# A decoder trunk with three attention groups on one core: a new order of mixing's steps, and joint slots for values and MLA results

## The chip, the core and the metric

The kernel runs as one program on one core of one Trainium2 chip. The metric is the device time of that program in microseconds (us), weights and input in device memory at its start, the result there at its end. Times of several runs are given as a median with the least and the greatest.

## What is computed

The input is 512 tokens of 1024 features in float32, and there are two layers. Each layer normalises its input, projects it once, and hands the columns to three groups of heads. The three outputs (512 + 256 + 256 features) go into one output projection, which is added to the input; an MLP of width 4096 with a squared ReLU follows, and after the last layer a final norm.

```python
for l in range(DEPTH):                                   # 2
    h = rmsnorm(x, g_mix[l])
    (cq, ckv, kr, aq, ak, av, qi, ki, wi, rq, rk, rv, rg) = jnp.split(h @ w_in[l], split_at, axis=-1)
    # MLA, 8 heads: low-rank queries (768) and keys/values (256), a shared rotary key, causal softmax
    q  = rmsnorm(cq, g_q[l]) @ w_uq[l]                   # 8 x (64 + 32 rotary)
    kv = rmsnorm(ckv, g_kv[l]) @ w_ukv[l]                # 8 x (64 key + 64 value)
    o_a = mla_attention(q_nope, q_rope, k_nope, k_rope, v_mla)
    # DSA, 4 heads, one key/value head: an indexer's score picks 128 causal keys per query
    score = einsum('bqh,bqhk->bqk', wi * idx_scale, relu(q_i . k_i))
    o_b = softmax over the keys of top_k(score, 128)
    # retention, 4 heads: decayed scores, group norm, swish gate
    o_c = silu(rg) * head_groupnorm(retention(q_c, k_c, rv), g_ret[l])
    x = x + concatenate([o_a, o_b, o_c]) @ w_out[l]
    x = x + square(relu(rmsnorm(x, g_mlp[l]) @ w_ff1[l])) @ w_ff2[l]
return rmsnorm(x, g_final)
```

## The kernel before

**Tiles.** Activations lie transposed, features on the 128 partitions and the 512 tokens along the free dimension, so a tile is 128x512 float32. Where the precision of float32 is wanted, a value is kept as a pair (high part and rest, both fp32r), and a product is three matmuls (`mm3`, the matmul itself at L146): high by high, rest by high and high by rest. Weights come from memory by DMA (tag "wr"), and `wsplit` makes the pair: ACT or POOL copies the high part (L192, L194), DVE or POOL subtracts (L215, L217). `gemm` is such a product over a list of contraction tiles, with the sum in one PSUM bank of tag "mm" (three of them); scores have three banks ("sc"), the products with values two ("o"). SBUF slots are shared by tag: 13 "g", 8 "qk", 8 pairs "u", 6 "p", 2 "v", one "sm". A tile of a tag waits until the slot's earlier tile has its last reader behind it.

**Who sets the order.** The kernel's Python emits instructions in program order, and a scheduler of the tile framework puts each on its engine's list by priority and by the readiness that it computes; `hp(k)` lowers or raises that priority for a kind of work by the table `PRI` (top-k rounds -225, results of the MLA -70, retention -44, `dm` +8, and so on). Program order in the mixing half of a layer is the string `ORDER`, whose words one loop hands to functions. The words are:

- `qi`, `tk`, `ix`: indexer queries, token tiles, index scores; they end in `accs`, three tables of 256, 384 and 512 keys. `t n` takes the next n jobs of the top-k queue: 48 rounds (`top_round`, L760 takes eight maxima, L761 replaces them; three tables, 16 rounds each), then three masks (L765).
- `rq`, `rk`, `rg`, `r n`: retention's queries, keys and gate, and the next n of its 16 scores.
- `aq`: DSA's queries. `dm` (`dsa_max`, scores L146, maxima L1110): the greatest score of each query and head over the masked keys; a transpose (L1114) and two small DMAs put it into a row of the queries, from which the exponentials are later taken. `d0` to `d3` (`dsa_block`, exponential L1159, results from L1133): the DSA blocks of 128 queries. They write `mix[4]` and `mix[5]`; retention writes `mix[6]` and `mix[7]`.
- `kv`, `kvf`, `kvc`: low-rank keys and values, their norm factor (L914) and the conversion. `cq`, `cqf`: low-rank queries and their factor. `mk`: slots of the keys, with the rotary key.
- `v0`, `v1` (`round_v`, copies out of PSUM L972): values of four heads each, from slots of tag "v". `rr0`, `rr1` (`round_rope`): the rotary part of a round's queries: a gemm, L978, a swap by DMA (L308), products (L143), a sum, a split.
- `k`, `q` (`pair_k`, `pair_q`): keys and queries of a pair of heads. The queries leave PSUM at L998, and four small DMAs (L1004) bring the rotary part of each head out of what `rr` left.
- `m` (`pair_max`, maxima L1025 and L1032): the greatest score of each query, as in `dm`.
- `a0` to `a7` (`pair_attn`, exponential L1093): one head each, four blocks of keys. The product with the values of a block is held back (`push`, four may be pending) so that scores go ahead of it; `F` flushes what is pending. When a pair's second head is done, `pair_done` copies the sums and products out of PSUM (L1050, L1052), takes the reciprocal by logarithm and exponential (L356, L357), corrects it, and writes the pair of `mix[gp]` (L1068) into a slot of tag "qk".

After the string comes OUT, the output projection: eight tiles of eight contraction tiles each, 192 matmuls, in the order 6, 7, 4, 5, 0, 1, 2, 3 of `mix`. The packing of the weight on the host (`mo`) has the same order. Then the MLP starts, for which the slots of "sm" and "v" are used too.

## Time and profile before

| | before |
|---|---|
| three runs, us | 1372.92, 1377.91, 1378.54 |
| median, us | 1377.91 |
| the profiled execution's own time, us | 1373.71 |
| its span, us | 1371.9 |
| mean granted clock of TensorE, of full | 0.979 |
| PE busy, us (7276 matmuls) | 1324.2 (97%) |
| weight loads (PEld) busy, us | 1100.4 (80%) |
| DVE busy, us (1744) | 1023.3 (75%) |
| ACT busy, us (1151) | 658.3 (48%) |
| POOL busy, us (263) | 268.9 (20%) |

The profile is of one execution; its starts and lengths are in us from the span's start. Its own time lies 1.8 us above its span. PE is TensorE's matmuls, DVE is VectorE, ACT is ScalarE, POOL is GpSimd, SP is the queue from which most DMAs are issued (SPq). Busy time of PE counts a matmul from its start to its modelled end, so two that follow each other overlap a little; the step from one start to the next is what it costs. [...]

### The profile page before, as it was taken

To read this page: it belongs to the slowest core of one execution; us is meant where nothing else is said; L and a number is where in the kernel's file an instruction comes from. 1 tells how busy PE (TensorE), PEld (TensorE's weight loads), DVE (VectorE), ACT (ScalarE), POOL (GpSimd) and SP (SyncE) were. 2 spreads that over 40 slices of the span, in tenths; PEclk is the share of its full clock that TensorE was granted. 3 is DMA by queue.
4 is the path that set the end of the run, shared out by engine and by line. 5 is a ranking of instruction groups with operands and counts; after the bars stand their busy time and mean duration, and the time that the engine had idled before them with its cause. 6 is when DMAs were issued, how large, how long until landed. Compare 5 with 4: busy or idle time off the path is not lost. (4 is left out here: it accounts for less than half of the span.)

```text
span 1371.9 us, 19881 instructions
## 1 busy us (share of the span) xinstructions
PE 1324.2 (97%) x7276; PEld 1100.4 (80%) x7276; DVE 1023.3 (75%) x1744; ACT 658.3 (48%) x1151; POOL 268.9 (20%) x263
## 2 busy tenths in 40 slices
PE   9999989999999999999998989899999999999997
PEld 7877765668888888899987767656778888889997
DVE  5799995555777776797759999756457776777875
ACT  4534433783444443465636345438644444445652
POOL 3456741004000000000033656311130000000000
PEclk9999997999999999999999998989999999999998
DMA  6668232203554555476555651221035555554652
GB/s 216 170 179 216 68 89 59 89 18 110 163 180 159 183 186 169 138 223 208 173 167 164 180 158 54 85 73 66 32 108 169 186 183 169 164 188 153 201 183 80
DMA packets 75777, 197.53 MB, mean 144 GB/s; under 512 B 8960, under 2 KB 13792, under 8 KB 75680
## 3 DMA queue, kind: packets, MB, share of 16 engines
q1 hardware_dynamic: 74528, 195.22, 46.1%
q8 instruction: 57, 0.93, 0.3%
q10 hardware_dynamic: 1152, 1.05, 0.2%
q14 instruction: 40, 0.33, 0.1%
HBM read 155.68 MB, written 20.97 MB: 129 GB/s over the span
## 5 line engine op out<-in xcount | busy, mean ns | idle before, releaser
L146 PE MATMUL mm<-u,wh 128*128 128x512 f32 (+1 forms) x1776 | 551.6, 390 | 0.0
L146 PEld LDWEIGHTS mm<-u,wh 128*128 128x128 f32 x1776 | 330.7, 189 | 64.6 <-issue 0.5
L146 PE MATMUL mm<-u,wl 128*128 128x512 f32 (+1 forms) x888 | 344.9, 388 | 0.1
L192 ACT ACTIVATE wh<-wr 128x512 fp32r<-128x512 f32 (+2 forms) x247 | 150.0, 610 | 296.9 <-PE mm L146 172.5
L215 DVE TENSOR_TENSOR wl<-wr,wh 128x512 fp32r<-128x512 f32 (+2 forms) x208 | 148.3, 714 | 84.1 <-ACT wh L192 83.1
L217 POOL TENSOR_TENSOR wl<-wr,wh 128x512 fp32r<-128x512 f32 (+2 forms) x80 | 102.9, 1287 | 489.5 <-ACT wh L192 405.5
L146 PEld LDWEIGHTS mm<-u,wl 128*128 128x128 f32 x888 | 167.8, 189 | 35.0 <-issue 0.7
L503 DVE TENSOR_TENSOR u<-wr,u 128x1024 fp32r<-128x1024 f32 x54 | 65.8, 1222 | 26.0 <-ACT u L502 25.8
L502 ACT ACTIVATE u<-wr 128x1024 fp32r<-128x1024 f32 x54 | 57.2, 1059 | 54.8 <-PE o L516 14.3
L445 DVE TENSOR_TENSOR sm<-wr 128x512 f32<-128x512 f32 x64 | 44.1, 690 | 47.5 <-DMA wr<-in_wff 47.5
L516 PEld LDWEIGHTS sc<-g,v 128*128 128x128 f32 x576 | 72.2, 189 | 2.3
L516 PE MATMUL sc<-g,v 128*128 128x256 f32 x576 | 73.1, 281 | 0.0
L146 PE MATMUL sc<-u,qk 97*128 97x512 f32 (+5 forms) x192 | 53.1, 393 | 3.6 <-ACT p L1093 3.6
L433 DVE SCALAR_TENSOR_TENSOR g<-mm,g 128x512 f32<-128x512 f32 x64 | 43.9, 686 | 14.7 <-PE mm L146 14.6
L194 POOL TENSOR_SCALAR wh<-wr 128x512 fp32r<-128x512 f32 (+3 forms) x41 | 28.9, 706 | 124.0 <-PE mm L146 60.5
L761 DVE MATCH_REPLACE8 g<-m,g 128x384 f32<-128x384 f32 (+2 forms) x96 | 51.3, 539 | 0.1
L342 PE MATMUL o<-p,v 128*128 128x256 f32 (+2 forms) x128 | 50.6, 499 | 0.0
L516 PE MATMUL o<-g,v 128*128 128x256 f32 x384 | 50.5, 281 | 0.0
L449 ACT ACTIVATE v<-wr 128x1024 fp32r<-128x1024 f32 x32 | 34.0, 1062 | 33.3 <-DVE wr L447 33.1
L760 DVE MAX8 m<-g 128x8 f32<-128x256 f32 (+2 forms) x96 | 49.9, 545 | 0.1
L516 PEld LDWEIGHTS o<-g,v 128*128 128x128 f32 x384 | 47.5, 189 | 0.0
L516 PE MATMUL sc<-wh,u 128*128 128x256 f32 x224 | 46.1, 285 | 0.8 <-DVE x L533 0.4
(299 smaller groups left out, 2631.8 us busy)
## 6 DMA issues: line engine op xcount, KB each, us to landing
wr<-in_wff SPq DMA_DIRECT2D x160, 512.0 KB
wr<-in_win SPq DMA_DIRECT2D x37, 512.0 KB
ws<-sm SPq DMA_DIRECT2D x32, 512.0 KB
wr<-ws SPq DMA_DIRECT2D x32, 512.0 KB
tab<-in_tabs SPq DMA_DIRECT2D x20, 512.0 KB
wr<-in_wout SPq DMA_DIRECT2D x16, 512.0 KB
p<-p SPq DMA_DIRECT2D x40, 128.0 KB
wr<-in_wuq SPq DMA_DIRECT2D x12, 384.0 KB
```

Source lines behind the costliest of these rows:

```text
L146: return nc.tensor.matmul(out, lhsT, rhs, start=start, stop=stop)
L192: return nc.scalar.activation(out, src, AF.Copy)
L215: order["wl"] = nc.vector.tensor_sub(lo, rc, R(hi))
L217: nc.gpsimd.tensor_sub(lo, rc, R(hi))
L342: nc.tensor.matmul(o[:, q0:], *terms[0], start=i == 0, stop=i == NB - 1, skip_group_check=True)
L433: nc.vector.scalar_tensor_tensor(r, ps, 0.0, rb, op0=ALU.max, op1=ALU.mult)
L445: nc.vector.tensor_add(sm[:, h], w[0], w[1])
L502: nc.scalar.activation(wh, t, AF.Copy)
L503: nc.vector.tensor_sub(wl, t, R(wh))
L516: nc.tensor.matmul(outs[m][0], a[:, m * P : m * P + P], b, start=i == 0 and outs[m][1] and n == 0, stop=i == KP - 1 and n == 2, skip_group ...
L760: nc.vector.max(m8, accs[j])
L761: nc.vector.match_replace(out=accs[j], in_to_replace=m8, in_values=accs[j], imm_value=GONE)
```

## The change

Three things change, and both layers have them. First, the string `ORDER`: the top-k jobs are handed out one or two at a time between the gemms, with what is left in one step behind `m2`; retention's scores come early; `aq1` and `aq0` stand behind `cq2`; `rr1`, `q2`, the heads `a2` and `a3` and `m2` stand ahead of `dm`; `dm` stands behind `k3` and directly ahead of `q3`; the DSA blocks come as `d3`, `d2`, `d1`, `d0` with the heads `a4`, `a5`, `a6` between them, and `a7` is last. Second, the slots: both rounds' values share one slot of tag "v"; the results of the first three MLA pairs share the other (`oss["mix"]`), and the fourth pair's goes to "sm". Third, OUT takes its contraction tiles in the order 6, 7, 0, 1, 2, 3, 4, 5, and the packed weight follows.

```diff
--- before.py
+++ after.py
@@ -51,7 +51,7 @@
 OPT_R = 0
 MHI = 'aaap'
 MLO = 'vp'
-ORDER = 'qi0 rg0 qi1 tk ix1 ix2 F rq0 ix3 rk0 rq1 r1 t2 r1 r1 t3 rk1 t4 rg1 aq1 r1 r1 aq0 F t2 t2 F F F F F t2 F F kv0 kv1 F F t1 F F r2 cq0 t2 t2 r1 r1 cq1 r4 kvf kvc t2 cq2 cq3 t5 r7 cq4 t1 t4 r16 t4 t2 cq5 r12 F F r6 r12 t1 F r2 v0 r16 r14 F r14 r9 cqf r2 t4 mk F t2 r1 r2 cqc r2 r2 r3 F t1 r11 rr0 t1 t4 t4 q0 r4 k1 t5 F k0 t2 r4 F t2 r2 q1 t4 r6 t4 r2 F t10 t10 t3 t4 m0 r2 r6 t2 r5 m1 r3 r2 r1 t3 t2 t5 a0 a1 t2 k2 t4 t4 dm t7 t4 r10 r1 t9 rr1 r1 t7 t3 r2 t4 a2 q2 a3 q3 t3 r3 m2 r7 t6 r10 r2 d2 t5 d3 d0 t15 d1 k3 t4 t2 r2 t2 t1 t3 m3 v1 a4 t8 t1 a6 F t3 r2 t4 t59 t2 r1 t6 r2 a7 r2 t3 t1 t3 a5 t2 t3 F r1 F r3 r2 r10 F r2 F'
+ORDER = 'qi0 rg0 qi1 tk ix1 ix2 F rq0 ix3 rk0 rq1 r1 r1 r1 rk1 rg1 t1 r1 r1 F kv0 kv1 t1 r2 cq0 t1 r1 r1 cq1 t1 r4 kvf kvc t1 cq2 t1 aq1 aq0 cq3 t1 r7 cq4 t1 cq5 t1 F cqf mk t1 v0 t2 rr0 t1 k0 t1 q0 t1 k1 t1 q1 t1 m0 t2 m1 t2 a0 t3 a1 t2 k2 t2 rr1 t2 q2 t3 a2 t3 a3 t3 m2 t59 k3 dm q3 d3 v1 m3 d2 a4 d1 a5 d0 a6 a7 F'
 PRI = {'fin': 0, 'w': 99, 'e': 59, 't': -225, 'rope': 0, 'split': 133, 'q': -16, 'qm': 0, 'rr': 0, 'v': 5, 'k': 0, 'att': 0, 'pv': 0, 'done': -70, 'ret': -44, 'st': 65, 'x': 0, 'tab': -20, 'cq': 0, 'tok': 15, 'idx': 0, 'dm': 8, 'rg': 0, 'km': 0, 'qi': 0, 'aq': 0}
 TOPK = 128
 NEG = -1e30
@@ -956,7 +956,10 @@
 
         def round_v(rd):
             with hp("v"):
-                v = v_([P, NB, 2, 192], F32)
+                if not vv:
+                    t = v_([P, 2, NB, 2, 192], F32)
+                    vv.update({"all": t})
+                v = vv["all"][:, rd]
                 for pr in range(2):
                     nc.gpsimd.memset(v[:, :, pr, 64:128], 1.0)
                 vv[rd] = v
@@ -1063,7 +1066,9 @@
                         rows = slice(64 * e, 64 * e + 64)
                         nc.vector.tensor_mul(y[rows], oss[gp, e][rows], y[rows])
                 nc.vector.scalar_tensor_tensor(s, s, 2.0, y, op0=ALU.subtract, op1=ALU.mult)
-                mt_ = qk_()
+                if gp == 0:
+                    oss["mix"] = v_([P, 3, 2, T])
+                mt_ = oss["mix"][:, gp] if gp < 3 else S("sm", 1, [P, 2, T], FR)
                 mh, ml = mt_[:, 0], mt_[:, 1]
                 nc.scalar.activation(mh, s, AF.Copy, scale=-1.0)
                 nc.vector.scalar_tensor_tensor(ml, s, -1.0, R(mh), op0=ALU.mult, op1=ALU.subtract)
@@ -1229,7 +1234,7 @@
             with after("aug") if OPT_X else nullcontext():
                 nc.sync.dma_start(x[n], xsrc[n])
         for n in range(KD):
-            ps = gemm(wout[l, n], (6, 7, 4, 5, 0, 1, 2, 3), mix)
+            ps = gemm(wout[l, n], (6, 7, 0, 1, 2, 3, 4, 5), mix)
             nc.vector.tensor_add(x[n], x[n], ps)
             sumsq_add(ss, x[n], n == 0, n == KD - 1)
         mode.update(hi="a", lo="v")
@@ -1334,7 +1339,7 @@
     wv = np.stack([f["w_ukv"][l][:, vcols].reshape(2, P, 2, 256).transpose(2, 1, 0, 3).reshape(2, P, 512)
                    for l in L])
     d["wukv"] = np.concatenate([wk, wv], 3)
-    mo = np.concatenate([np.arange(t * P, (t + 1) * P) for t in (6, 7, 4, 5, 0, 1, 2, 3)])
+    mo = np.concatenate([np.arange(t * P, (t + 1) * P) for t in (6, 7, 0, 1, 2, 3, 4, 5)])
     d["wout"] = np.stack([_pack(f["w_out"][l][mo]) for l in L])
     d["wff1"] = np.stack([_pack(f["w_ff1"][l]) for l in L])
     rows = np.concatenate([np.arange(t * P, (t + 1) * P) for t in (0, 1, 4, 5, 2, 3, 6, 7)])
```

The number of instructions on each engine is the same. A line of the kernel before at or behind L962 is 3 further on in the changed kernel, from L1069 on 5 (L998 is L1001 there). Where the new order moves them, three places show. Names are those of the program's tiles, with a running number that differs between the two; a row is line, operation, written tile <- read tiles, and shape of the moving or written data.

The first is PE in layer 0 inside `dm`. `sc` <- `km` is a DSA score, the matmul with `ma` and `cbt` behind it adds the mask; `mm` <- `x` or `u` is a product of queries. Before:

```order
L146 MATMUL sc_2252<-km_293,qk_1125 128x512
L146 LDWEIGHTS cbt
L146 MATMUL sc_2252<-ma_450_1941,cbt 128x512
L146 MATMUL sc_2256<-km_293,qk_1125 128x512
L146 LDWEIGHTS cbt
L146 MATMUL sc_2256<-ma_450_1941,cbt 128x512
L342 MATMUL o_2323<-p_2180,v_1785 128x256
L146 MATMUL sc_2260<-km_293,qk_1055 128x512
L146 LDWEIGHTS cbt
L146 MATMUL sc_2260<-ma_450_1941,cbt 128x512
L342 MATMUL o_2323<-p_2180,v_1785 128x256
```
And the change, at the fifth and sixth score since `dm`'s start and what follows; `mm_2498` is the sum of `q3`:

```order
L146 MATMUL sc_2438<-km_293,qk_1449 128x256
L146 LDWEIGHTS cbt
L146 MATMUL sc_2438<-ma_557_2402,cbt 128x256
L146 MATMUL sc_2438<-km_293,qk_1449 128x256
L146 LDWEIGHTS cbt
L146 MATMUL sc_2438<-ma_557_2402,cbt 128x256
L146 MATMUL mm_2498<-x_1191,wh_2490 128x512 x2
L146 MATMUL mm_2498<-x_1191,wl_2491 128x512
L146 MATMUL sc_2444<-km_293,qk_1395 128x256
L146 LDWEIGHTS cbt
L146 MATMUL sc_2444<-ma_557_2402,cbt 128x256
```
Before, scores and masks alternate, with a product of `p` and `v` (the first MLA heads) between; products of queries come at its end. Now six scores with their masks stand first, and from there three matmuls of `q3` come between scores.

The second is DVE in layer 0, at the end of the top-k rounds. `MAX` and `MATCH_REPLACE` are a round's two halves, the `tiny` rows are `pair_max`. Before, behind the first two evictions of queries (L998); the one instruction of these rounds that stands further ahead, between the evictions and this piece, is the `MAX` of `m_446`:

```order
L1025 TENSOR_REDUCE tiny_2098<-sc_2113 128x2
L1032 TENSOR_REDUCE tiny_2098<-sc_2119 128x1
L1032 TENSOR_REDUCE tiny_2098<-sc_2123 128x1
L215 TENSOR_TENSOR wl_2439<-wr_2436,wh_2438 128x384
L760 MAX m_447_1934<-g_761 128x8
L761 MATCH_REPLACE g_666<-m_446_1931,g_666 128x384
L761 MATCH_REPLACE g_761<-m_447_1934,g_761 128x512
L765 TENSOR_SCALAR ma_449_1939<-g_666 128x384
L765 TENSOR_SCALAR ma_450_1941<-g_761 128x512
```
And the change, where L1001 is that eviction:

```order
L143 TENSOR_TENSOR p_1787<-p_1787 128x512
L765 TENSOR_SCALAR ma_557_2402<-g_624 128x256
L761 MATCH_REPLACE g_666<-m_555_2396,g_666 128x384
L761 MATCH_REPLACE g_761<-m_556_2399,g_761 128x512
L238 TENSOR_TENSOR g_1826<-p_1787,g_1825 128x512
L1001 TENSOR_TENSOR g_1881<-mm_1862,g_1714 128x512
L1001 TENSOR_TENSOR g_1947<-mm_1928,g_1714 128x512
L765 TENSOR_SCALAR ma_558_2404<-g_666 128x384
```
All rounds and one of the masks now stand ahead of the first two evictions; before, four halves of rounds and two masks stood behind them.

The third is PE in layer 0 where the output projection first stands. Before, `mm_2979` is its first sum:

```order
L146 MATMUL sc_2844<-u_2467,qk_1864 128x256 x2
L146 LDWEIGHTS cbt
L146 MATMUL sc_2844<-cbt 128x128
L146 MATMUL sc_2844<-u_2467,qk_1865 128x256
L342 MATMUL o_2835<-p_2798,v_2698 128x256 x2
L146 MATMUL mm_2979<-u_1456,wh_2971 128x512
L146 MATMUL sc_2852<-u_2467,qk_1864 128x256 x2
L146 LDWEIGHTS cbt
L146 MATMUL sc_2852<-cbt 128x256
L146 MATMUL sc_2852<-u_2467,qk_1865 128x256
L342 MATMUL o_2863<-p_2833,v_2698 128x512
```
And the change, where `mm_2616` is a sum of `v1`, and `mm_2976` and `mm_3013` are the first two sums of OUT, ahead of a score of the block d3 (`sc_2535`):

```order
L146 MATMUL mm_2616<-wl_2589,g_1344 128x256
L146 MATMUL mm_2616<-wh_2588,g_1345 128x256
L146 MATMUL mm_2976<-u_1300,wh_2968 128x512 x2
L146 MATMUL mm_2976<-u_1300,wl_2969 128x512
L146 MATMUL mm_2976<-u_1692,wh_2968 128x512 x2
L146 MATMUL mm_2976<-u_1692,wl_2969 128x512
L146 MATMUL mm_2976<-v_2284,wh_2968 128x512 x2
L146 MATMUL mm_2976<-v_2284,wl_2969 128x512
L146 MATMUL mm_3013<-u_1300,wh_3005 128x512
L146 MATMUL sc_2535<-qk_1450,km_293 128x256
L146 MATMUL sc_2535<-qk_1395,km_295 128x256
```
Before, one matmul of OUT stands among the scores of the fourth pair's first head (row `mm_2979`), and the rest behind the last head. Now 10 stand directly behind `v1` and 7 more among the scores of d3, ahead of the DSA blocks d2 to d0 and the fifth to eighth head.

## Rows read from the trace of the kernel before

**Rows 1.** The page: busy time by engine; granted clock in 40 slices, in tenths.
```profile
PE 1324.2 (97%) x7276; PEld 1100.4 (80%) x7276; DVE 1023.3 (75%) x1744; ACT 658.3 (48%) x1151; POOL 268.9 (20%) x263
...
PEclk9999997999999999999999998989999999999998
```

**Rows 2.** Stretches of mixing: us, busy time by engine, granted clock, DMA share, GB/s.
```profile
60.00:193.90 133.90, 121.67 (x534) 94.45 (x532) 132.08 (x268) 61.30 (x121) 84.85 (x81) 0.99 0.54 150
207.40:214.90 7.50, 7.50 (x43) 5.21 (x41) 3.84 (x10) 4.53 (x10) 0.00 (x0) 1.00 0.61 176
214.90:237.50 22.60, 22.60 (x57) 10.88 (x56) 11.58 (x18) 5.81 (x11) 4.16 (x5) 0.62 0.04 13
217.80:234.90 17.10, 17.10 (x33) 7.29 (x33) 7.58 (x12) 2.84 (x5) 0.00 (x0) 0.50 0.05 16
237.50:250.90 13.40, 13.40 (x76) 9.48 (x75) 7.14 (x12) 6.70 (x16) 0.98 (x2) 1.00 0.52 167
250.90:305.00 54.10, 50.73 (x253) 34.36 (x251) 30.02 (x53) 46.20 (x94) 3.81 (x4) 1.00 0.10 32
735.00:868.90 133.90, 122.70 (x524) 94.92 (x524) 129.11 (x265) 60.32 (x119) 79.06 (x76) 0.96 0.50 140
810.00:835.00 25.00, 21.48 (x79) 16.02 (x78) 21.93 (x49) 11.19 (x22) 16.93 (x17) 0.80 0.16 50
890.30:910.70 20.40, 20.40 (x52) 9.61 (x52) 10.54 (x17) 5.00 (x10) 2.24 (x3) 0.67 0.04 14
928.10:981.80 53.70, 50.52 (x252) 34.28 (x251) 29.26 (x52) 46.07 (x94) 2.83 (x3) 1.00 0.09 28
```

**Rows 3.** PE's timeline, layer 0, after the queries: start us, us, instruction, idle before.
```profile
193.89 1.13 PE L146 MATMUL mm<-x,wh 128*128 128x512 f32 x2 [4.46 <-DVE g L998]
```

**Rows 4.** DVE's groups by line and shape: the top-k rounds (busy us, mean ns).
```profile
L760 DVE MAX8 m<-g 128x8 f32<-128x512 f32 x32 | 21.7, 678 | 0.0
L761 DVE MATCH_REPLACE8 g<-m,g 128x512 f32<-128x512 f32 x32 | 21.5, 672 | 0.0
...
L760 DVE MAX8 m<-g 128x8 f32<-128x384 f32 x32 | 17.4, 544 | 0.0
L761 DVE MATCH_REPLACE8 g<-m,g 128x384 f32<-128x384 f32 x32 | 17.2, 539 | 0.0
```

**Rows 5.** PE's timeline, layer 1, at the kv factor.
```profile
822.29 1.09 PE L271 MATMUL sc<-cft,tiny 128*128 128x128 f32 x4 [3.52 <-DVE tiny L914]
```

**Rows 6.** PE's timeline where the output projection starts in each layer.
```profile
297.96 0.58 PE L146 MATMUL mm<-u,wh 128*128 128x512 f32 x1
...
298.61 0.62 PE L146 MATMUL mm<-u,wh 128*128 128x512 f32 x2
...
302.06 0.62 PE L146 MATMUL mm<-u,wh 128*128 128x512 f32 x2
...
974.77 0.58 PE L146 MATMUL mm<-u,wh 128*128 128x512 f32 x1
```

**Rows 7.** ACT's groups from 250.9 to 305, by line and shape.
```profile
L1050 ACT ACTIVATE g<-o 64x512 f32<-64x512 f32 x5 | 3.0, 592 | 0.1
...
L357 ACT ACTIVATE g<-g 64x512 f32<-64x512 f32 x4 | 2.5, 627 | 0.1
...
L1068 ACT ACTIVATE qk<-g 128x512 fp32r<-128x512 f32 x4 | 2.4, 622 | 2.3 <-DVE g L1065 2.3
...
L972 ACT ACTIVATE v<-mm 128x256 f32<-128x256 f32 x4 | 1.5, 379 | 0.6 <-PE mm L146 0.6
```

**Rows 8.** Timelines of SP, POOL, PE: rope of round 1, first product of `m2`.
```profile
211.91 1.17 SPq L308 DMA_DIRECT2D p<-p  x2
...
214.98 1.27 POOL L143 TENSOR_TENSOR p<-p,tab 128x512 f32<-128x512 f32 x1 [11.23 <-DMA p<-p]
...
229.03 3.04 SPq L1004 DMA_DIRECT2D u<-g  x4
...
244.62 0.47 PE L146 MATMUL sc<-qk,u 96*128 96x256 f32 x1
```

## The prediction, made before the changed kernel had run

> **What bounds the kernel now.** The page comes first [rows 1]: TensorE (PE) is busy 97% of the span, so whatever the change brings must come out of PE's waits and out of the time in which PE runs at the lower of its two clock levels. The page's slices of 34.3 us then show where the low clock is: in the 7th, 25th and 27th, all of them in mixing (the last slice aside, where the program ends). In the MLPs PE simply streams. So I cut mixing into stretches and read busy times and granted clock for each. [rows 2] holds three different regimes, and the reader should see that no one average describes them.
>
> First, up to the second pair's queries, VectorE (DVE) is the limit: 132.1 us busy of 133.9 in layer 0, 129.1 of 133.9 in layer 1. At its end PE stands 4.46 us for the DVE instruction that takes the queries out of PSUM [rows 3]. Second, the DSA maxima (step `dm`, 214.9 to 237.5): PE counts as busy all 22.6 us, yet the granted clock averages 0.62; in layer 1 0.67 over 20.4 us. [...] Third, from the first DSA exponential to the last MLA result, ScalarE (ACT) is the limit: 46.2 us busy in 54.1, 46.1 in 53.7, with PE waiting for its exponentials in between.
>
> **The DVE regime: the top-k does not move back.** The step list hands out its rounds later, but the excerpts of DVE's order show where they land: ahead of layer 0's first eviction of queries (L998 before, L1001 now) stand all 96 maxima and replacements of that layer, where it was 92 before. Two maxima and two replacements more, of 384 and 512 elements, cost 2 x 0.54 + 2 x 0.67 = 2.4 us [rows 4]; I take 2.3 because consecutive DVE rows overlap a little. Since DVE is full there, this delays PE by as much: **+2.3 us per layer**. Bounds: 0, if DVE's 1.8 to 4.8 us of idle time take them up, and +6, if the new order of retention and `aq` leaves DVE waiting as long again as it does now in layer 1. Layer 1 has something to win in return. PE waits 3.52 us for the kv factor at 822.3 [rows 5], and the stretch around it runs at 0.80 with DVE idle 3.1 of 25 us. With the two `aq` tiles behind `cq2`, `kvf` has, by the order, some 14 us less DVE work ahead of it and 11 us less of PE's (48 matmuls of 0.23). I count half of those 3.1 us as regained: -1.5 (bounds 0 and -3.1). Sum here +2.3 and +0.8.
>
> **The rest, counted from the first score of `a0`** (207.4 and 882.9). A 512-column matmul steps by 0.23 us: 15 of them from 298.61 to 302.06 [rows 6]. OUT has 192 in a layer. Before, one is done early; the other 191 start at 297.96 and 974.77 and need 43.9 us, so OUT ends 134.5 and 135.8 us after `a0`. Now the same for the changed order, step by step:
>
> - `a0` to `a3`, `m2`, `k3`. `a0` and `a1` take 7.5 us [rows 2]. `a2`, `a3` and `m2` take 13.4, less nine matmuls of `q3` (2.1) and one DSA score (1.0) that lie in that row: 10.3. Four matmuls of `q2` and six of `k3`: 2.3. The eight value products of `a1` and `a3`, which stood elsewhere: 2.5, an estimate of two passes over 512, 384, 256 and 256 columns at the rate of [rows 6]. Together 22.6.
> - `dm`, now woven with `q3`, `v1` and the first of OUT. `dm` alone: 22.6 us at 0.62 is 14.0 at full clock, less 14 matmuls of q (3.2) and `a1`'s products (1.25): 9.6. Then 18 of `q3` 4.1, 24 half-wide ones of `v1` 2.8, 13 of OUT 3.0, and two thirds of three DSA scores 1.5: 21.0 at full clock.
> - The clock there. The trace has no `dm` with gemms woven through it. Nearest rows: `dm` nearly alone loses 8.6 us (22.6 - 14.0), and the next stretch, `a2` to `m2` with `q3` mixed in, loses nothing (1.00). I take **3 us**: `dm` still opens with six pairs in a row, and in layer 0 the low clock began within 4 us of such a start, lasted 17.1 us and ended when q's gemms came [rows 2]. Bounds 0 and 21 (half clock throughout).
> - The ACT regime. It starts 22.6 + 21.0 + 3 = 46.6 us after `a0`. By ACT's order 14 of its 94 instructions now stand ahead of it: four splits of queries and two copies for `a3`, all of 64x512 out of PSUM (0.59 each), four evictions of `v1` (0.38), the logarithm and exponential of `a3`, and two results [rows 7]. That is 3.5 + 1.5 + 1.3 + 1.2 = 7.5 us of 46.2. At the same ratio of busy to elapsed the 54.1 us become 54.1 x 38.7/46.2 = **45.3** (bounds: 40, with ACT nearly full, and 50, if it waits for PE more). PE has about 36 us of work in it, among it 28 matmuls of OUT that need no fourth pair, since OUT's order of products now ends 0, 1, 2, 3, 4, 5. DSA's four blocks are finished before the last head, and being read last they hold nothing up. The fourth pair's result is there 91.9 us after `a0`.
> - OUT's last 147 matmuls: 33.8. It ends **125.7** us after `a0`.
>
> That is 8.8 and 10.1 us sooner, 18.9 in all; less the 3.1 of the DVE regime, **16 us**.
>
> **What costs nothing.** The joint slot for both rounds' values lets `v1` start without waiting for a slot of its own; it is hidden by `q3` beside it. Results in the "v" and "sm" slots instead of "qk": "sm" is wanted again by the MLP only after its first two tiles. Without that cover the MLP's first sums would wait for OUT's last 6 matmuls, 1.4 us. The same instructions are issued, DMAs included; on SP the eight small loads of `rr1` now stand ahead of the next wout loads and the x loads, and the latter have 40 us to land.
>
> **The rivals.**
> 1. *The clock at `dm` stays as it is.* Then 8.6 and 6.7 us are lost instead of 3 each, and the gain shrinks by 9.3. Against it: the clock rose in [rows 2] as soon as gemms were mixed in. For it: those first six pairs. Time: 16 - 9.3, so 1368 on the basis below. [...] Chance 0.22.
> 2. *The low clock swallows the gemms: slower.* If it falls in `dm`'s opening pairs and doesn't rise, then `q3`, `v1` and OUT's first products, which were all at full clock, run at half: up to 21 us instead of 3, or 18 more per layer. From 11 us per layer on the change loses. Time: 1359 + 36 = 1395. For it: the low clock lasted those 17.1 us once entered. Against: it ended with gemms in the mixture. Chance 0.10.
> 3. *`m2` waits for `rr1`'s rope: about no change.* `m2` comes some 17 us after `a0` now; in the trace its first product starts at 244.62, 37 us after [rows 8]. There the rope runs: DMA at 211.9, multiplication at 214.98, loads into the queries from 229.0 to 232.1, which is 25 us after `a0`, because nothing hurried it. The bare chain (DMA 3.1, product 1.3, sum and split 2, four loads 3, landing 2) would end 15 us after. If it is as late as it was, PE stands 8 us in each layer, and the 16 us are gone. It decides from 17 us on. Chance 0.10.
> 4. *The step list says more than it does.* The tail stays ACT-bound as long as before (50 us or more) and the DVE regime grows by 6: within 0.5%. Chance 0.06.
>
> **How the numbers follow.** The sum stands on the profiled execution, 1373.7 us with a span of 1371.9; it gives 1357.7. The median of the runs shown is 1377.9, 4.2 above it, and would give 1362. I say **1359**. My forecast, a gain of 8 to 28 us, has 0.52. The range of 8 in 10 runs from 1342 (no clock loss at `dm`, ACT nearly full) to 1378 (rivals 1, 3 and 4); rival 2 lies outside. A measurement of this kernel can tell about 0.5%, 7 us. Faster by more: 0.52, two thirds of rival 1, and a little of 3: 0.69. Within: the rest of 1, most of 3 and 4: 0.18. Slower: rival 2 and the bad ends of 3: 0.13.
>
> **What would show it.** Right: granted clock above 0.8 from `m2` to the first DSA exponential; the stretch from that exponential to the last result near 45 us; 17 matmuls of OUT ahead of the last heads; OUT's end some 126 us after `a0`; PE's wait for the queries a little over 4.5 us. Wrong: a clock near 0.6 through `q3` and `v1` (rival 2), a PE wait at `m2`'s first product (rival 3), or an ACT stretch of over 50 us (rival 4). The forecast falls if `a0` starts more than 6 us later than it does now, or if OUT ends more than 132 us after it.

## The result, and the profile after

| | before | changed |
|---|---|---|
| median of 13 runs each, us | 1376.24 | 1383.06 |
| ratio to before, 95% interval | | 1.0065 [1.0041, 1.0089] |
| profiled execution: span, us | 1371.9 | 1380.6 |
| profiled execution: granted clock | 0.979 | 0.983 |

The change makes the kernel 0.65% slower; 16 us faster was forecast. The ratio is formed over fast executions, without one of before that took 2131.8 us; it is not the quotient of the two medians, from which it differs by up to 0.3% here and in the table further down. The profile's page of the changed kernel, busy time by engine and the clock in 40 slices, answers to [rows 1]:

```profile
PE 1321.3 (96%) x7274; PEld 1100.3 (80%) x7276; DVE 1028.4 (74%) x1744; ACT 657.8 (48%) x1151; POOL 269.7 (20%) x263
...
PEclk9999989999999999999999999999999999999998
```

The 7 and the two 8s that stood in mixing are gone, one 8 stands a slice ahead of where the 7 was, and still the span is 8.7 us longer. To see where, both traces are cut at the same five places: the first score of `a0` (what lies ahead of it I call the front, what lies behind it the tail), the statistics of the MLP (the first matmul behind the output projection, OUT) and the end of layer 0, then again in layer 1. Columns as in [rows 2]; first before:

```profile
0.00:207.40 207.40, 193.91 (x910) 153.35 (x911) 182.63 (x354) 93.38 (x185) 108.72 (x109) 0.98 0.55 155
207.40:345.90 138.50, 134.27 (x595) 92.02 (x593) 76.47 (x120) 80.57 (x155) 28.07 (x27) 0.94 0.23 72
345.90:686.20 340.30, 339.09 (x2153) 307.85 (x2153) 257.91 (x402) 164.04 (x252) 3.25 (x3) 1.00 0.56 179
686.20:882.80 196.60, 181.78 (x865) 145.93 (x865) 171.16 (x348) 83.42 (x169) 101.06 (x98) 0.97 0.48 134
882.80:1022.70 139.90, 135.60 (x606) 93.50 (x606) 76.76 (x118) 80.84 (x156) 27.80 (x26) 0.95 0.24 75
```

and the changed kernel:

```profile
0.00:216.80 216.80, 199.47 (x912) 156.03 (x913) 184.44 (x361) 93.40 (x185) 107.66 (x109) 0.95 0.53 151
216.80:351.50 134.70, 128.12 (x594) 89.40 (x593) 76.70 (x113) 80.03 (x155) 28.68 (x27) 1.00 0.22 70
351.50:692.80 341.30, 339.39 (x2152) 307.83 (x2153) 257.95 (x402) 163.83 (x252) 3.25 (x3) 1.00 0.55 178
692.80:895.70 202.90, 185.86 (x876) 149.21 (x877) 174.40 (x353) 84.04 (x170) 101.75 (x98) 0.96 0.48 135
895.70:1030.70 135.00, 128.18 (x594) 89.41 (x593) 76.70 (x113) 80.02 (x155) 28.34 (x26) 1.00 0.22 69
```

The reader should see two things. `a0` starts 9.4 us later in layer 0 and 6.3 us later in layer 1 (I forecast 2.3 and 0.8). And from `a0` on the clock is 1.00 where it was 0.94 and 0.95, yet these stretches shrink by 3.8 and 4.9 us only (forecast: 8.8 and 10.1). The two MLPs take 1.0 and 0.7 us more. One thing in these rows is easily missed. In layer 1 the cut at `a0` does not divide the same work: 865 matmuls lie ahead of it before and 876 after, 606 and 594 behind it. Eleven products of queries have changed sides, some 2.5 us at 0.23 each, so that much of the late `a0` there, and of the shorter tail, is no loss and no gain.

**A second measure.** Cut into 2743 windows of half a microsecond, the profiled execution of before has a granted clock of 1.00 in 2622 of them, of 0.50 in 109, and between the two in 12. I take a microsecond at the lower clock to do half the work. (Two passes through `dm` in one execution, shown below, bear it out: 17.80 us at 0.62, which is 11.0, against 11.90 at 1.00.) So a length times its mean clock is about what it would take at full clock, as long as PE has work; I call that *time by clock*. What the clock took is the rest. Summed over the windows of half a microsecond in which the clock was below full, the lower clock cost the profiled execution of before 29.0 us and that of the changed kernel 23.5, so time by clock went from 1342.9 to 1357.1: **14.2 us of waiting or work more, 5.5 us of clock less**. Every run lists span and clock, and there it is the same: the medians of time by clock are 1343.6 us (before, 32 runs beside the first experiments) and 1357.5 (changed, 13 runs). It is the steadier of the two: over the four lots of runs beside the experiments the executions of before go from 1360 us at 0.989 to 1383 at 0.974, and their time by clock stays between 1340 and 1348, with the medians 1343.6, 1344.7, 1343.1 and 1343.9. (The clock is listed to 0.001, so a single run's value is good to 0.7 us. Between kernels of different lots a difference of less than 2 us by clock is not shown, since those of before differ by 1.6.)

### The profile page after: what moved, and what is told of

The parts are those of the page before. It is cut to its first block, busy times and chain, and to the rows that moved or that the text cites. A ratio compares the mean times of both kernels' runs of the same rounds, so it can differ in the third digit from the quotient of the medians.

```text
span 1380.6 us, 19881 instructions
## 1 busy us (share of the span) xinstructions
PE 1321.3 (96%) x7274; PEld 1100.3 (80%) x7276; DVE 1028.4 (74%) x1744; ACT 657.8 (48%) x1151; POOL 269.7 (20%) x263
## 4 chain that ended last, share of the span: by engine, by line
PE 77%; DVE 11%; ACT 5%; issue 3%; DMA 2%; POOL 1%; POOLq 0%; SPq 0%; DVEq 0%; ACTq 0%
PE mm L146 43%; PE sc L516 11%; PE sc L146 7%; PE mm L516 6%; PE o L516 5%; PE o L342 2%; PE o L146 2%; DVE wl L215 1%; DVE p L143 1%; DMA p<-p 1%; DVE g L753 1%; DVE m L760 1%; DVE g L761 1%; ACT g L1150 1%; POOL p L143 1%
## 5 line engine op out<-in xcount | busy, mean ns | idle before, releaser
L192 ACT ACTIVATE wh<-wr 128x512 fp32r<-128x512 f32 (+3 forms) x247 | 149.8, 610 | 305.3 <-PE mm L146 195.3
L215 DVE TENSOR_TENSOR wl<-wr,wh 128x512 fp32r<-128x512 f32 (+2 forms) x208 | 154.5, 744 | 91.6 <-ACT wh L192 90.8
L217 POOL TENSOR_TENSOR wl<-wr,wh 128x512 fp32r<-128x512 f32 (+3 forms) x80 | 103.3, 1291 | 521.6 <-ACT wh L192 492.0
L146 PE MATMUL sc<-u,qk 97*128 97x512 f32 (+5 forms) x192 | 61.4, 418 | 0.3 <-ACT p L1098 0.2
L761 DVE MATCH_REPLACE8 g<-m,g 128x512 f32<-128x512 f32 (+2 forms) x96 | 51.4, 539 | 0.1
L342 PE MATMUL o<-p,v 128*128 128x256 f32 (+2 forms) x128 | 46.8, 462 | 3.6 <-ACT g L1055 3.6
L146 PE MATMUL mm<-x,wh 128*128 128x512 f32 x96 | 38.0, 474 | 11.9 <-DVE g L1001 11.7
```

Of the source, the lines that this page charges most:

```text
L146: return nc.tensor.matmul(out, lhsT, rhs, start=start, stop=stop)
L192: return nc.scalar.activation(out, src, AF.Copy)
L215: order["wl"] = nc.vector.tensor_sub(lo, rc, R(hi))
L217: nc.gpsimd.tensor_sub(lo, rc, R(hi))
L342: nc.tensor.matmul(o[:, q0:], *terms[0], start=i == 0, stop=i == NB - 1, skip_group_check=True)
L761: nc.vector.match_replace(out=accs[j], in_to_replace=m8, in_values=accs[j], imm_value=GONE)
```

## The experiments

**Theories.** *Sum*: the new string's front (up to `a1`) makes `a0` late, its tail saves clock in `dm`, and both are independent. Rivals: the joint slots or OUT's order do it; or the two halves interact. Edits of the step string are shown by the words that change. All medians stand in one table behind the experiments.

**Four cuts.** The front alone, the tail alone (with the slots and OUT's order), the slots and OUT's order alone, the string alone.

`e1_front`:

```diff
-ORDER = old up to a1, old from a1
+ORDER = new up to a1, "t51", old from a1
```

> Kernel before with the new step string up to the step a1 only; tail, slots and order of products as before. Theory (the two halves of the string add up): a0 starts as late as in the changed kernel, 9.4 us later in layer 0 and some 6 us later in layer 1, nothing is won behind it, so 12 to 17 us slower than before. Rival (the delay of a0 comes from what the new tail or the joint slots make DMA queues and buffers do): a0 within 2 us of before, no change.

`e2_tail`:

```diff
-ORDER = new up to a1, new from a1
+ORDER = old up to a1, new from a1
```

> Changed kernel with the old step string up to the step a1. Theory: a0 starts as before (207.4 us), the granted clock stays 1.00 through dm, and a0 to the statistics of the MLP takes 134 to 135 us in each layer instead of 138.5 and 139.9: 7 to 10 us faster than before. Rival (the clock stayed up only because DVE had finished the masks long before): clock under 0.8 in dm, within 4 us of before.

`e3_slots`, the changed kernel with the whole old string, and `e4_order`, the kernel before with the whole new one:

```diff
-ORDER = new                (changed kernel)
+ORDER = old                (e3_slots)
-ORDER = old                (kernel before)
+ORDER = new                (e4_order)
```

> Changed kernel with the whole old step string: only the joint slots and the new order of the output projection's products are left. Theory: no change, within 3 us of before. Rival (the slots or the order of the products hold back the MLP, which took 1.1 and 0.7 us longer in the changed kernel): 2 us slower or more, to be seen behind the output projection.

> Kernel before with the whole new step string, slots and order of products as before. Theory (the string does nearly all): as slow as the changed kernel, 5 to 10 us over before; the output projection starts behind the last head only, which costs up to 4 us more per layer. Rival (the new order needs the joint slots): v1 waits for a slot of its own, over 15 us slower than before.

Measured: `e1_front` 1.0006 [0.9978, 1.0035], `e2_tail` 1.0008 [0.9973, 1.0043], `e3_slots` 1.0014 [0.9983, 1.0044], none of which is clear of no change, and `e4_order` 1.0120 [1.0080, 1.0159]. Slots and OUT's order do nothing with the old string (time by clock 1343.4 against 1343.6), but the new string needs them: without them its time by clock is 1361.6, with them 1357.5. In the profile of `e1_front` `a0` is late (216.3 and 203.6 us into the layers, as in the changed kernel), and still no loss is shown; the 12 to 17 us that were expected did not come. The *old* tail behind it took 130.0 and 130.7 us instead of 138.5 and 139.9, in both layers:

```profile
216.30:346.30 130.00, 125.78 (x591) 88.51 (x589) 73.32 (x112) 80.37 (x155) 27.95 (x27) 1.00 0.23 72
891.00:1021.70 130.70, 126.52 (x594) 89.11 (x592) 73.32 (x112) 80.49 (x155) 27.79 (x26) 1.00 0.23 72
```

Its `dm` ran at full clock, in one row of the windows:

```profile
223.70:239.00 15.30, 15.30 (x56) 8.20 (x56) 11.34 (x18) 5.91 (x12) 2.25 (x3) 1.00 0.11 36
```

against 0.62 over 22.6 us in [rows 2]. Nothing in the instructions explains it. PE's timeline opens `dm` in the same way in the kernel before:

```profile
214.89 0.38 PE L146 MATMUL sc<-km,qk 64*128 64x256 f32 x1
215.20 0.28 PE L146 MATMUL sc<-cbt 128*128 128x256 bf16 x1
215.42 0.38 PE L146 MATMUL sc<-km,qk 64*128 64x256 f32 x1
215.73 0.28 PE L146 MATMUL sc<-cbt 128*128 128x256 bf16 x1
```

and in `e1_front`:

```profile
223.76 0.38 PE L146 MATMUL sc<-km,qk 64*128 64x256 f32 x1
224.07 0.28 PE L146 MATMUL sc<-cbt 128*128 128x256 bf16 x1
224.28 0.38 PE L146 MATMUL sc<-km,qk 64*128 64x256 f32 x1
224.60 0.28 PE L146 MATMUL sc<-cbt 128*128 128x256 bf16 x1
```

A score with its mask takes 0.53 us in both; the clock falls 2.9 us behind the first score in the one and not in the other. One execution can have both: in `e3_slots`, the same 42 matmuls of `dm` in layer 0 and layer 1,

```profile
221.50:239.30 17.80, 17.80 (x42) 7.71 (x41) 9.66 (x15) 2.82 (x6) 2.24 (x3) 0.62 0.05 16
895.00:906.90 11.90, 11.90 (x42) 5.70 (x41) 9.38 (x15) 2.66 (x5) 2.24 (x3) 1.00 0.02 6
```

So the low clock in the old `dm` is a thing that a pass through it may or may not have. Five profiled kernels have it without gemms between its scores (before, `e1_front`, `e3_slots`, and `g4_dmback` and `h1_aqlate` below); in six of their ten passes the clock fell, and the profile that the prediction was made from had it in both layers. The rows also show that PE is not as busy as its share says: a 512-column matmul steps by 0.23 us [rows 6], these of 256 columns by 0.31 and 0.21, at full clock. In the changed kernel's `dm` the same mask steps by 0.04 us where a gemm follows it and by 0.21 where a score does, so PE stands behind the mask, which the modelled ends of the matmuls cover; for what it stands is not shown. It also follows that the new tail has nothing over the old one but the clock: with nearly the same matmuls (594 in each layer of the changed kernel, 591 and 594 here) and at full clock in `dm` it takes 134.7 and 135.0 us, the old one 130.0 and 130.7 (less what the clock took, layer 0 of before, `e3_slots` and `h1_aqlate` has 130.0, 130.4 and 129.5). By clock the front costs 7.6 us (1351.2 - 1343.6) and the tail 9.0 (1352.6 - 1343.6); together 16.6, and the changed kernel has 13.9. The clock's gains don't add up likewise: what it took is 29 us before, 25 with the front, 18 with the tail, 23 with both (median span times one less the clock). The theory of independent halves holds for the work to within 2.7 us and falls for the clock.

**How late `a0` is, over all profiles.** One profile does not tell it. With the old front (before, `e2_tail`, `e3_slots`, and `g3_dmq2` below) `a0` of layer 0 starts at 207.4, 207.9, 214.1 and 213.1 us, and less what the clock took ahead of it at 204.0, 204.5, 203.8 and 204.5. With the new front (changed, `e1_front`, `e4_order`, and `f3_blocks`, `g1_out`, `g4_dmback` below) it starts at 214.7 to 220.5 and by this count at 205.1 to 207.8. So the new front costs some 2 us of work in layer 0, and the rest of the 9.4 us is clock, of which the profile of before had little. In both layers' fronts together the clock took 8.5 to 18.7 us with the old one and 17.0 to 23.9 with the new.

**What in the tail costs.** `f3_blocks` has the DSA blocks together again, `g1_out` the old order of OUT, `g4_dmback` `dm` in its old place, all else as changed.

```diff
-... k3 dm q3 d3 v1 m3 d2 a4 d1 a5 d0 a6 a7 F
+... k3 dm q3 v1 m3 d2 d3 d0 d1 a4 a6 F a7 a5 F        (f3_blocks)
-ps = gemm(wout[l, n], (6, 7, 0, 1, 2, 3, 4, 5), mix)
+ps = gemm(wout[l, n], (6, 7, 4, 5, 0, 1, 2, 3), mix)  (g1_out; the packing likewise)
-... k2 t2 rr1 t2 q2 t3 a2 t3 a3 t3 m2 t59 k3 dm q3 d3 ...
+... k2 t59 dm rr1 q2 a2 a3 m2 k3 q3 d3 ...            (g4_dmback)
```

> Changed kernel with the DSA blocks together again and the heads after them, a4 a6 a7 a5, dm and all before it in the new places. Theory (the weave of DSA blocks and heads makes three accumulations share the two PSUM banks of products, which costs the waits of 0.96 and 0.85 us for L1055, and puts the last two pairs' results at the end): these waits vanish, a0 to the statistics 131 to 133 us instead of 134.7 and 135.0, 4 to 8 us faster than the changed kernel. Rival (the heads in front of dm are what costs): a0 to the statistics stays at 134 to 136, no change.

> Changed kernel with the output projection's products back in the order 6, 7, 4, 5, 0, 1, 2, 3 (slots and step string as changed). Theory (a part of the tail's loss is that the projection reads the pairs' results before DSA's and so stands 1.68, 0.24 and 0.77 us for them): these waits fall under 0.5 us in all, a0 to the statistics 132 to 133 us, 3 to 5 us faster than the changed kernel (1378 to 1380). Rival (the DSA results are as late as the pairs'): a0 to the statistics 134.5 or more, no change.

> Changed kernel with dm back behind k2, all else of the new string kept. Theory (the late dm is what makes the new tail longer at full clock, because the DSA blocks and the last heads come in one crowd behind it): time by clock 4 to 8 us under the changed kernel's 1357.5; with the clock low in dm in some executions 1374 to 1382. Rival (it is the weave of blocks and heads, or the last heads' order): time by clock within 2 us of 1357.5.

Measured: `f3_blocks` 1389.6 us (four runs), a0 to the statistics 139.1 (3.4 of it clock): the theory falls. Undoing the weave of blocks and heads wins nothing; whether the weave is worth the 2.4 us by clock and 6 in time that lie between the two is not shown, as the intervals overlap. `g1_out` 1390.4 us, 140.0 and 139.7 (1.7 clock, and eleven more matmuls between `a0` and the statistics than in the changed kernel): it falls too. The waits for the pairs' results went, and a longer one for DSA's came, in PE's timeline:

```profile
310.83 1.25 PE L146 MATMUL mm<-g,wh 128*128 128x512 f32 x3 [2.93 <-ACT g L1150]
```

So OUT's order, and perhaps the weave, repays a little of what the late `dm` costs. `g4_dmback` shows that cost and its gain at once. By clock it takes 1352.9 us, 4.6 less than the changed kernel, as the theory said (why a late `dm` costs work is not shown: the crowd behind it, which the theory names, was not tested by itself); but its clock is the worst of all, 0.970 to 0.973 in each of five runs, and it is the slowest, 1395.1 us, 1.0149 [1.0123, 1.0175]. `dm` in its windows, both layers:

```profile
226.50:249.00 22.50, 22.50 (x55) 10.87 (x55) 10.97 (x18) 5.91 (x11) 4.17 (x5) 0.62 0.04 13
910.00:932.00 22.00, 22.00 (x62) 10.91 (x61) 9.90 (x16) 5.94 (x12) 3.20 (x5) 0.69 0.08 24
```

PE counts as busy all the time, with few instructions, at three quarters and two thirds in the lower clock, as in [rows 2]. With gemms between its scores the clock stays up as a rule: of the ten profiled kernels with the woven `dm` nine have full clock there in both layers, and that of `h2_keys`, below, had 0.51 for 21 us in layer 1. That is one pass of twenty, against six of ten without them.

**What in the front costs.** Two parts are undone in the changed kernel, one done alone in the kernel before.

```diff
-... rk1 rg1 t1 r1 r1 F kv0 ... cq2 t1 aq1 aq0 cq3
+... rk1 rg1 aq1 aq0 t1 r1 r1 F kv0 ... cq2 t1 cq3     (f2_aq, in the changed kernel)
-... rg1 aq1 r1 r1 aq0 F ... cq2 cq3
+... rg1 r1 r1 F ... cq2 aq1 aq0 cq3                   (h1_aqlate, in the kernel before)
-... cq5 t1 F cqf mk t1 v0 t2 rr0 t1 k0 t1 q0 t1 k1 t1 q1
+... cq5 t1 F v0 t1 cqf mk t2 rr0 t1 q0 t1 k1 t1 k0 t1 q1   (h2_keys, in the changed kernel)
```

> Changed kernel with aq1 and aq0 back behind rg1. Theory (the front's loss is DSA's query tiles, put among the low-rank tiles where VectorE is needed): a0 6 to 9 us earlier in layer 0 and 4 to 6 in layer 1, 6 to 10 us faster than the changed kernel (1373 to 1377). Rival (the loss comes from the new order of keys, values and queries or of retention): a0 within 2 us of the changed kernel, 1381 to 1385.

> Kernel before with aq1 and aq0 moved behind cq2, nothing else. Theory (of the new string's front, DSA's query tiles among the low-rank tiles are the larger half of the loss; putting them back won 4.9 us of the changed kernel): 3 to 7 us slower than before, a0 2 to 4 us later in each layer. Rival (they cost only together with the new order of keys, values and queries): within 2 us of before.

> Changed kernel with v0 ahead of cqf and mk, and q0 k1 k0 q1 in the old order. Theory (v0's products behind the factor of the queries are what PE waits for with 1.17 and 2.67 us at 167 to 171 us, followed by a stretch of low clock): these two waits fall under 2 us in all, the low clock at 170 us goes, 4 to 8 us faster than the changed kernel (1375 to 1379). Rival (the queue of evictions behind PE is as long in either order): within 2 us of it.

`h1_aqlate` has 1.0055 [1.0021, 1.0089] and 1348.8 us by clock: DSA's query tiles among the low-rank tiles, alone, cost 5 us by clock, of 7.6 for the whole front. Putting them back in the changed kernel gives 1378.2 us; the 4.9 us between the medians are not shown to be a gain, since the ratios are 1.0043 and 1.0065 with intervals that overlap, and by clock the difference is 1.5. `h2_keys` gives 1378.3 too, but its profile still has the waits that were to go (0.96 and 2.68 us at 172 and 176), so that theory is not borne out; whether it won anything stays open, as its interval, [1.0011, 1.0068], overlaps that of the change. What the rest of the front costs, and by which wait, is open too.

**Is DVE the limit ahead of `a0`?** The prediction took it so. Then work taken from it must bring `a0` forward. Nine rounds (of 48) and the three masks are issued behind the second pair's queries, in the changed kernel (`f5_hold9`), in `e2_tail` (`f6_e2hold9`), and in that with OUT's old order (`g2_e2hold9out`):

```diff
+                        held = q is fill_top and len(q) <= HOLD + NB - 1     # HOLD = 9
+                        if held and "qe" not in order:
+                            break
                         f, *a = q.popleft()
-                        f(*a)
+                        with after("qe") if held else nullcontext():          # behind pair_q(1)'s eviction
+                            f(*a)
...                                                                            # "qe" is that eviction
```

> Changed kernel with the last nine top-k rounds (three of each table, 18 halves, about 10 us of VectorE) issued behind the second pair's eviction of queries. Theory (VectorE sets the start of a0, and the new step list did not move the rounds): a0 8 to 10 us earlier in each layer, dm ends 40 to 44 us after a0, 13 to 20 us faster than the changed kernel (1363 to 1370). Rival (a0 is set by something else, or the masks now come late): a0 within 3 us, or dm ends 50 us after a0; 1378 to 1386.

> The same hold of nine rounds on the kernel with the old step string up to a1 and the new tail (e2_tail, 1372). Theory: a0 8 to 10 us earlier in each layer, 12 to 18 us faster than e2_tail: 1354 to 1361, faster than the kernel before by 1 per cent or more. Rival: as in f5_hold9, 1368 to 1376.

> Old step string up to a1, new tail, nine rounds held behind the queries (f6_e2hold9) and the old order of the projection's products. Theory: g1's gain on top of f6's, 1362 to 1366, faster than the kernel before by 0.5 to 1 per cent. Rival: no gain, 1367 to 1371.

In `f5_hold9` `a0` came 5.6 us earlier in layer 0 and 1.6 in layer 1 (201.3 us into it, against 202.9), for 10 us less of DVE's work in each; all but some 2 us of that, in layer 0, is clock (6.8 us lost ahead of `a0` in each layer, against 10.2 and 8.5). In `f6_e2hold9` (209.6 and 201.5 us, against 207.9 and 193.9 in `e2_tail`) it was no earlier. The times are 1377.3 and 1368.7 us, by clock 1.4 and 2.6 us less than without the hold, where 13 to 20 and 12 to 18 were expected. `g2_e2hold9out` lost it again (1378.0), with OUT's waits as in `g1_out`. DVE's timeline of `f5_hold9` ahead of the eviction (L1007 there) shows what took the place of the rounds:

```profile
185.07 0.69 DVE L987 TENSOR_TENSOR p<-mm,g 128x512 f32<-128x512 f32 x1 [0.71 <-ACT g L273]
186.73 1.21 DVE L854 SCALAR_TENSOR_TENSOR g<-g,gn,g 128x512 f32<-128x512 f32 x1 [0.97 <-POOL g L853]
...
190.01 0.69 DVE L239 TENSOR_TENSOR u<-g,u 128x512 fp32r<-128x512 f32 x1 [1.47 <-ACT u L193]
...
194.60 0.69 DVE L144 TENSOR_TENSOR p<-p 128x512 f32<-128x512 f32 x1 [1.15 <-POOL p L144]
...
195.99 0.75 DVE L239 TENSOR_TENSOR g<-p,g 128x512 fp32r<-128x512 f32 x1 [0.23 <-ACT g L193]
196.77 1.29 DVE L1007 TENSOR_TENSOR g<-mm,g 128x512 f32<-128x512 f32 x2
```

The eviction that PE waits for stands in DVE's queue behind the rope of round 0 (L987, L144, L239), and that is a chain through ACT, a DMA and POOL. With the rounds gone DVE stands in it: 24.4 us busy in the 32 from 180, and PE still waits 4.41 us at the eviction.

**A version that beats both.** The old tail is the shorter one if the clock stays up, and the gemms of `rr1` and `q2` and one head ahead of `dm` may do for that:

```diff
-... a1 t2 k2 ... dm ... rr1 ... a2 q2 a3 q3 m2 d2 d3 d0 d1 k3 m3 v1 a4 a6 F a7 a5 F
+... a1 t2 k2 rr1 a2 q2 dm a3 q3 m2 d2 d3 d0 d1 k3 m3 v1 a4 a6 F a7 a5 F        (g3_dmq2)
+... a1 t2 k2 rr1 a2 q2 t51 dm a3 ..., and six rounds held as above              (h3_dmq2hold)
```

> Kernel before with rr1, a2 and q2 ahead of dm, the rest of the tail in the old order, old slots and products. Theory (the old tail takes 130 us when the clock stays up, and gemms of queries around dm keep it up): no low clock in dm, a0 to the statistics 130 to 132 us, time by clock as before (1343 to 1346), 1358 to 1366. Rival (any step put ahead of dm costs what the new tail costs): a0 to the statistics 133 or more at full clock, time by clock 1348 or more, no faster than 1370.

> g3_dmq2 (1368.6) with six top-k rounds issued behind the second pair's queries. Theory (as with f6_e2hold9 against e2_tail): 2 to 5 us faster than g3_dmq2, 1363 to 1367, 0.6 to 0.9 per cent faster than before. Rival (dm stands too near and waits for the masks): 1369 to 1376.

`g3_dmq2`, on the kernel before: 1368.6 us, **0.9956** [0.9931, 0.9982]; `h3_dmq2hold`: 1362.0 us, **0.9931** [0.9899, 0.9963], 1345.0 by clock at 0.989. From `a0` to behind `dm` in the latter's windows, both layers:

```profile
207.30:235.10 27.80, 27.55 (x118) 16.41 (x118) 21.60 (x43) 12.84 (x26) 4.35 (x5) 1.00 0.21 63
894.80:922.00 27.20, 26.95 (x135) 17.13 (x134) 16.84 (x27) 13.54 (x25) 4.36 (x5) 1.00 0.38 123
```

Full clock in both, and a0 to the statistics takes 131.6 us in each: the old tail's length to 1 or 2 us, at the new tail's clock. The gain is clock alone: by clock neither takes less than before (1346.9 and 1345.0, against 1343.1 and 1343.9 beside them). What the hold adds is not shown by the ratios, whose intervals overlap.

| | median us | ratio to before | clock, median | time by clock, median |
|---|---|---|---|---|
| before (four lots) | 1372.2 to 1374.2 | 1 | 0.979 to 0.980 | 1343.1 to 1344.7 |
| changed | 1383.1 | 1.0065 | 0.983 | 1357.5 |
| e1_front | 1378.7 | 1.0006 | 0.982 | 1351.2 |
| e2_tail | 1372.3 | 1.0008 | 0.987 | 1352.6 |
| e3_slots | 1376.1 | 1.0014 | 0.978 | 1343.4 |
| e4_order | 1390.1 | 1.0120 | 0.980 | 1361.6 |
| f2_aq | 1378.2 | 1.0043 | 0.985 | 1356.0 |
| f3_blocks | 1389.6 | 1.0111 | 0.980 | 1359.9 |
| f5_hold9 | 1377.3 | 1.0022 | 0.986 | 1356.1 |
| f6_e2hold9 | 1368.7 | 0.9969 | 0.988 | 1350.0 |
| g1_out | 1390.4 | 1.0124 | 0.979 | 1359.6 |
| g2_e2hold9out | 1378.0 | 1.0017 | 0.982 | 1351.6 |
| g3_dmq2 | 1368.6 | 0.9956 | 0.985 | 1346.9 |
| g4_dmback | 1395.1 | 1.0149 | 0.971 | 1352.9 |
| h1_aqlate | 1377.9 | 1.0055 | 0.980 | 1348.8 |
| h2_keys | 1378.3 | 1.0039 | 0.986 | 1355.6 |
| h3_dmq2hold | 1362.0 | 0.9931 | 0.989 | 1345.0 |

## Why the prediction was wrong, point by point

Two terms of the sum failed: the front's 3.1 us, and the new tail's 125.7. Between the two profiles the forecast is off by 24.5 us. The front has 12.6 of them (15.7 late, 3.1 forecast), 8.5 of which are clock. The tails have 10.2: 16.2 us more work than I had, less 6.0 of clock that they saved beyond the forecast. The MLPs, which I took as unchanged, have 1.7. Both signs that I named for the forecast's fall came: `a0` 9.4 and 6.3 us late, and OUT's end 133.7 us behind it in both layers.

- **"Up to the second pair's queries, DVE is the limit."** This is the step that failed in the front. 132.1 us busy of 133.9 [rows 2] says that DVE had no room, not that it held PE up: ten us less of its work moved `a0` by some 2 us and by nothing, clock aside (`f5_hold9`). In the changed kernel DVE did 134.7 us in 142.4, so 2.6 us more work (forecast 2.4) and **5.9 us more of standing**:

```profile
60.00:202.40 142.40, 126.33 (x534) 96.53 (x532) 134.71 (x274) 61.30 (x121) 82.85 (x81) 0.94 0.52 145
```

  PE's timeline shows the larger waits there, against [rows 3] and the one of 3.52 us in [rows 5], which did go:

```profile
87.86 0.79 PE L146 MATMUL sc<-qk,qk 128*128 128x512 f32 x1 [2.12 <-DMA qk<-g]
...
170.77 0.58 PE L146 MATMUL mm<-wh,g 128*128 128x256 f32 x1 [2.67 <-ACT g L279]
...
202.36 1.19 PE L146 MATMUL mm<-x,wh 128*128 128x512 f32 x2 [6.22 <-DVE g L1001]
...
881.11 1.19 PE L146 MATMUL mm<-x,wh 128*128 128x512 f32 x2 [5.52 <-DVE g L1001]
```

  and the windows around those in layer 0 show the low clock that begins in each of them:

```profile
87.50:95.00 7.50, 7.13 (x15) 4.13 (x15) 6.00 (x15) 3.14 (x6) 2.51 (x3) 0.54 0.70 189
169.50:176.50 7.00, 5.73 (x17) 4.86 (x18) 5.03 (x13) 3.18 (x7) 4.01 (x4) 0.51 0.70 158
200.00:207.50 7.50, 5.14 (x15) 3.76 (x15) 5.56 (x11) 2.93 (x5) 0.64 (x2) 0.54 0.34 119
```

  Each of the three came with some 3.4 us of clock. That is no fixed price. The fronts of the two profiles have twelve waits of 2 us or more; two were followed by no low clock, five by 1.7 us of loss, four by 3.4 and one by 5.1. The wait of one and the same score in the kernel before, in layer 0 and in layer 1, each with its windows:

```profile
71.30 0.80 PE L146 MATMUL sc<-g,v 96*128 96x512 f32 x1 [2.22 <-ACT g L748]
69.00:76.00 7.00, 4.78 (x15) 3.77 (x15) 7.00 (x12) 4.80 (x10) 1.48 (x2) 0.76 0.62 169
743.82 0.50 PE L146 MATMUL sc<-g,v 96*128 96x512 f32 x1 [2.16 <-ACT g L748]
741.50:748.50 7.00, 4.84 (x21) 3.39 (x21) 7.00 (x12) 5.76 (x11) 1.08 (x3) 1.00 0.70 187
```

  Of the 9.4 us by which `a0` is late in layer 0, 6.8 are clock (10.2 against 3.4) and 2.6 the rest, which is near the 2.3 that I had, though for another reason; in layer 1 it is 1.7 and 4.6, and 2.5 of the 4.6 are the eleven matmuls that changed sides. I had counted the front's waits one by one and never what each does to the clock.
- **"The top-k does not move back": right.** All rounds ran ahead of the queries, at the pace of before (71 halves by 170 us, 76 before).
- **"The clock there: I take 3 us."** The direction was right and the size on the good side: none was lost in the woven `dm`, and `g4_dmback` brings the loss back; rival 1 did not come. That the gain came near the 9.3 us forecast has luck in it: I took before as losing 15.3 us there each time and the change as losing 6, while the five profiles of the old `dm` lose 9 on average (0 to 15) and the woven one nothing in 19 passes of 20. And the 22.60 us busy of 22.60 [rows 2] say less than they seem to: they cover the small waits behind the masks (0.21 us to a score, where a gemm follows after 0.04). With gemms between the scores the clock stayed up in 19 of 20 passes, without them in four of ten; what makes it fall there is not shown. In the front each of the three low stretches above begins in a wait, of 2.12, 2.67 and 6.22 us.
- **"The rest": the larger term that was mis-sized is the new tail itself.** I had it 3 us shorter than the old one at full clock in layer 0 (125.7 less 3, against 134.5 less 8.6); it is 4 to 5 us longer (134.7 and 135.0 to the statistics, against 130.0 and 130.7 in `e1_front`). ACT's timeline gives the first DSA exponential, and the fourth pair's result:

```profile
265.45 2.26 ACT L1164 ACTIVATE p<-sc 128x512 f32<-128x512 f32 x4
...
313.83 0.63 ACT L1073 ACTIVATE sm<-g 128x512 fp32r<-128x512 f32 x1 [0.33 <-DVE g L1068]
```

  The first is 48.7 us behind `a0`, where I had 46.6 with 3 of clock in it: 5.1 us that I had not counted, 1.1 of them PE's waits. From there to the result it takes 49.0, where I scaled ACT's share to 45.3. The windows show that ACT was not the limit any more:

```profile
265.40:314.50 49.10, 44.47 (x207) 28.42 (x205) 23.74 (x44) 39.12 (x80) 1.58 (x2) 1.00 0.03 12
```

  ACT 39.1 of 49.1, as counted (38.7), but PE 44.5, where I had put 36; the rest is PE's waits, as for the pairs' results at 309.74 and 314.52 (1.68 and 0.77 us). PE was at 50.7 of 54.1 before too, in the row from which I named ACT [rows 2]. An OUT matmul steps by 0.246 us over the whole of it (47.0 us for 191), not 0.23; this is 3 us before and 2 us after and nearly cancels.
- **"What costs nothing": right** for the slots (`e3_slots`), and slots and OUT's order hide more than I said: 4 us by clock with the new string (`e4_order`), of which the order is 2 (`g1_out`).
- **Rivals 2 to 4.** None of them is what came. `m2` did not wait for `rr1`'s rope (it ended 23.1 us behind `a0`, with no wait). The end on the slower side came from the front, 9.4 us late in layer 0 where I had bounded it at 6, together with tails that came out 10.2 us longer than forecast. Rival 4 came nearest, with a front 6 us later and an ACT stretch of 50 us or more (measured: 49), and I put it at no change.

## What to carry to other kernels

A busy share close to one on an engine that has other work to fill its time with doesn't make it the limit: take work from it and see whether the waiting engine moves. Where the clock changes from run to run, compare length times granted clock, and give the clock its own line in the sum: in these fronts a wait of 2 us or more on TensorE cost 0 to 5 us more by clock. Before counting a low stretch as a gain, see in several profiles how often it is there (here six passes of ten). If a sparse stretch of matmuls loses the clock, try the few gemms at hand around it before moving whole stages (here it stayed up in 19 passes of 20 with gemms between the scores, in four of ten without). And when two profiles are cut at the same instruction, compare the counts of instructions on both sides before comparing the lengths.

## What the runs showed of the hardware

The same instructions, the masked scores of `dm`, ran at a granted clock of 0.62 in one layer and 1.00 in the other of one execution (`e3_slots`), with PE counted as busy throughout in both; the 42 matmuls took 17.80 and 11.90 us. The same wait of 2.2 us in the kernel before was followed by low clock in one layer and not in the other. Executions of the kernel before spread over 1.7% (1360 to 1383 us), mostly with the clock (0.972 to 0.990), while length times clock stays between 1340 and 1348. Where the clock moved is kept for one execution of each kernel only; why it differs from run to run is not shown.
